# Five units of seven products in the second feed-forward layer, with three sums of weights made in DRAM and the fourth on VectorE

## The chip, the cores and the metric

The kernel runs on one core of a Trainium2 chip. The metric is the device time of one execution in microseconds; the time shown is the median of the runs. Below, PE is TensorE, DVE VectorE, ACT ScalarE, POOL GpSimd, SP SyncE.

## The reference

A bidirectional encoder trunk of two layers on an input of 256 positions by 2048 features, in float32. The first layer mixes by pooling and grouped attention, the second by an mLSTM; each is followed by a gated feed-forward part, which is what the change touches:

```python
D_MODEL = 2048; SEQ = 256; DEPTH = 2; D_FF = 5632

def conv_ffn(x, w_up, conv_w, conv_b, w_down):
    u = x @ w_up                                   # 256 x 2048 by 2048 x 11264
    up = jnp.pad(u, ((0, 0), (1, 1), (0, 0)))
    c = conv_w.astype(u.dtype)
    u = c[0] * up[:, :-2] + c[1] * up[:, 1:-1] + c[2] * up[:, 2:] + conv_b.astype(u.dtype)
    gate, val = jnp.split(u, 2, axis=-1)
    return (jax.nn.silu(gate) * val) @ w_down      # 256 x 5632 by 5632 x 2048

for layer in range(DEPTH):
    h = rms_norm(x, norm_mix[layer])
    ...                                            # attention (layer 0) or mLSTM (layer 1)
    x = x + mixed
    x = x + conv_ffn(rms_norm(x, norm_ffn[layer]), w_up[layer], conv_w[layer], conv_b[layer], w_down[layer])
```

## The kernel before

**Products in two halves.** Every float32 product is made of two-part numbers: activations and weights are each split into a high part (a cast to `fp32r`) and a low part (the rest), and PE makes high x high, high x low and low x high.

**The stream of weights.** All weights stand in one list, `weights`, in the order in which PE uses them. An entry, here called a chunk, is a tile of 128 x 1024 float32, 512 KB. `Stream.load` issues the DMA of the next chunk on SP's queue into a buffer `w`; `Stream.split` makes from it the tile `hl`, with a cast on ACT (L164) and a subtraction on DVE (L165). In a feed-forward layer there are seven buffers `w`, loaded up to seven chunks ahead, and five buffers `hl`, split up to three chunks ahead; the fifth buffer is a pool of its own, used by the chunks whose number leaves 4 when divided by 5. PE's order is the order in which the code is written; that of DVE, ACT, POOL and the DMA queues is set by a scheduler which plays the program through with times of its own, except for instructions that are pinned to their order (`keep_in_program_order`).

**A feed-forward layer.** The 5632 hidden features are 44 tiles of 128, in six groups `c` (`FCH`: 4, 8, 8, 8, 8, 8 tiles). `_ffn_plan` writes the order: an up step `n` (one chunk, 16 matmuls of the tile `up`; four steps make one hidden tile), a down step `d` (one chunk, 12 matmuls, tile `dn`), and a step `s` of a unit. Down steps of group `c - 1` alternate with the up steps of group `c`. A chunk is used by one step, so the steps of a layer number its chunks.

**A unit of seven products.** For four hidden tiles at once (with gate and value, a matrix of 2048 by 1024) `quads` uses the scheme in which a 2 x 2 block product takes seven multiplications instead of eight. It goes through the 16 row blocks of the weights in eight pairs; a pair has four blocks of 128 x 512, called b11, b12, b22 and b21, and needs four sums:

- b11 + b12,
- b12 + b22,
- b22 + (b11 + b12),
- b21 + that.

A unit takes 28 chunks and steps of six matmuls each (tiles `p`; 168 matmuls of 512 columns): 16 in a first pass with two chunks a pair, 12 in a second pass with three chunks for two pairs. PE multiplies sums of the activations (tile `sx`, made by DVE and ACT as each layer begins) and sums of the weights. At its end `finish` transposes the four results (tile `tr`, four transposes for each hidden tile, so 16 in a unit) and passes them to `tail`, the convolution and gate on ACT and DVE.

**Where the sums are made.** `UNITS` lists for each layer the units: group `c`, half of the group, first and last slot (a slot is one step that is not of a unit), and `made`. With `made` 1, all four sums are made in DRAM ahead of time: `make_step` copies the pair's four blocks into a DRAM tile `G` (two copies of 512 KB on SP) and then lets POOL issue accumulating DMAs, two that add from the weights and two within `G`, 256 KB each. Chunks of the unit are then loaded from `G`. With `made` 0, DVE adds in the buffer `w` (`sums`, L144 to L150), four additions of 128 x 512 for each pair. The lists `places` say at the load of which chunk each of a pair's four steps is issued. In each layer the units (2,1), (3,1) and (5,1) have `made` 1 and (4,1) has 0.

Of the kernel before, what the change touches and what calls it, by code (L numbers as in the profile page):

```python
# [64 lines left out]
class Stream:  # L65
# [46 lines left out]
    def make_step(self, key, part, src):  # L112

        pin, sync, add = self.tc.keep_in_program_order, self.nc.sync, self.nc.gpsimd
        G = self.made_tile(key)
        if part < 2:
            r = slice(64 * part, 64 * part + 64)
            pin(sync.dma_start(G[r], src[r]))
            pin(add.dma_start(G[r, 0:1024], src[r, 512:1536], accum_op=ALU.add))  # L119
# [5 lines left out]
    def prepare(self, kind, w):  # L125

        if kind[1] == 0:
            self.first = w
            return
        x, G = self.first, self.made_tile(kind[2])  # L130
        pin, add = self.tc.keep_in_program_order, self.nc.vector.tensor_add
        b11, b12, b22, b21 = (e[:, c : c + 512] for e in (x, w) for c in (0, 512))
        for to, other in ((b11, b12), (b12, b22), (b22, b11), (b21, b22)):
            pin(add(to, to, other))
        self.nc.gpsimd.dma_start(G[:, 0:1024], x)
        self.nc.gpsimd.dma_start(G[:, 1024:2048], w)
# [16 lines left out]
    def split(self, then=None):  # L153
        i = self.n_split
        self.sums(i)
        w, n, width, kind = self.w.pop(i)[:4]
        if isinstance(kind, tuple):
            self.prepare(kind, w)
            self.n_split += 1
            self.sums(i + 1)  # L160
            return
# [18 lines left out]
    def next(self):  # L180
        while self.is_prep(self.at):
            self.at += 1
        i = self.at
        self.ahead(i)
        self.at += 1
        return self.hl.pop(i)

    def is_prep(self, i):
        return isinstance(self.srcs[i], tuple) and isinstance(self.srcs[i][0], tuple)
# [1052 lines left out]
def _down_chunks(w):  # L1242
# [10 lines left out]
    ((2, 1, 18, 57, 1), (3, 1, 64, 90, 1), (4, 1, 97, 141, 0), (5, 1, 148, 174, 1)),  # L1253
# [41 lines left out]
def _ffn_order(layer, up, dn, four, last):  # L1295
# [4 lines left out]
    for step in _ffn_plan(layer):  # L1300
# [7 lines left out]
        else:  # L1308
# [7 lines left out]
            if n >= 2 * m:  # L1316
                seq.append(("made", ((key, 1, 2), q[:, 1024:1536])) if made else ("left", q[:, 512:1536]))
# [7 lines left out]
def _pairs(layer, four):  # L1325
    return [(f"{layer}{c}{h}_{p}", four[u, p]) for u, (c, h, _, _, made) in enumerate(UNITS[layer]) if made
            for p in range(KT // 2)]


def _with_prep(seq, pairs, first, gap):  # L1330

    out = []
    for i, e in enumerate(seq):
        n, r = divmod(i - first, gap)
        if r == 0 and 0 <= n < len(pairs):
            key, q = pairs[n]
            out += [(("prep", 0, key), q[:, 0:1024]), (("prep", 1, key), q[:, 1024:2048])]
        out.append(e)
    return out


def _make_steps(make, pairs, places):

    for (key, q), (at, gap) in zip(pairs, places):
        for part in range(4):
            make.setdefault(at + part * gap, []).append((key, part, q))
# [109 lines left out]
```

## Time and profile before

| | |
|---|---|
| time, median of 3 runs | 2171.28 us (2171.19 to 2171.61) |
| the profiled execution | 2171.85 us, span 2170.1 us |
| PE busy | 2162.6 us, 100% of the span |
| weight loads on PE busy | 1838.7 us, 85% |
| DVE busy | 1679.4 us, 77% |
| ACT busy | 1285.1 us, 59% |
| POOL busy | 185.5 us, 9% |
| moved by DMA | 566.76 MB, mean 261 GB/s |
| granted PE clock | 1.0 |

The times are microseconds from the start of the span. In the trace's answers a row of the timeline gives start, duration, engine, line, operation, the tiles written and read, and the count; what stands in brackets is the idle time before it and what ended it. A row of the windows gives for a stretch of time its length, then the busy time of each engine with the number of instructions, the granted clock, the share of time in which the DMA engines were busy, and the GB/s they moved. Durations of matmuls overlap, since they are pipelined.

The first feed-forward layer is on PE from 256 to 971 us, the mLSTM layer from there to 1449 us, the second feed-forward layer from 1449 us to the end.

### The profile page before, as it was taken

The numbers are of one execution on the slowest core, as the hardware profiler recorded it, in microseconds if no ns is written. First come the engines' busy times: TensorE is split into PE (matmuls) and PEld (weight loads), VectorE is DVE, ScalarE is ACT, GpSimd is POOL, SyncE is SP. The second block draws the span as 40 slices with busy tenths as digits, with TensorE's granted clock in tenths as the row PEclk, the third lists the DMA queues.
The fourth block names the chain that finished last, engine by engine and source line by source line (L and its number), as shares of the span: only waits on it lengthen the run. The fifth ranks groups of instructions, "written<-read, shape, count | busy, mean of one in ns | idle before, by whom it ended". The sixth has DMA issues, their size and how long they took to land.

```text
span 2170.1 us, 30692 instructions
## 1 busy us (share of the span) xinstructions
PE 2162.6 (100%) x11040; PEld 1838.7 (85%) x11040; DVE 1679.4 (77%) x2350; ACT 1285.1 (59%) x1808; POOL 185.5 (9%) x232
## 2 busy tenths in 40 slices
PE   9999999999999999999999999999999999999999
PEld 7888888888888888889888888888888888788887
DVE  7686698787798787866767676769878778878785
ACT  7665565666665566655555454556566665557663
POOL 1121111110101000001111010110000000000000
PEclk9999999999999999999999999999999999999999
DMA  8878889999989978879788887888998997776873
GB/s 325 250 221 254 260 266 341 343 295 313 322 273 306 302 221 255 262 212 254 216 257 228 237 242 224 265 231 250 290 284 268 305 309 241 257 233 223 253 235 125
DMA packets 170268, 566.76 MB, mean 261 GB/s; under 512 B 20762, under 2 KB 23106, under 8 KB 168578
## 3 DMA queue, kind: packets, MB, share of 16 engines
q1 hardware_dynamic: 145376, 510.44, 68.3%
q0 software_dynamic: 21664, 50.61, 15.2%
q10 hardware_dynamic: 3074, 3.75, 0.8%
q8 instruction: 86, 1.41, 0.3%
q14 instruction: 68, 0.56, 0.1%
HBM read 562.57 MB, written 102.80 MB: 307 GB/s over the span
## 4 chain that ended last, share of the span: by engine, by line
PE 98%; DVE 1%; issue 0%; ACT 0%; DMA 0%; ACTq 0%; DVEq 0%
PE up L285 28%; PE dn L285 21%; PE p L285 14%; PE op L285 8%; PE mv L285 4%; PE mq L285 4%; PE mk L285 4%; PE mo L285 4%; PE qproj L285 3%; PE pool L285 1%; PE kproj L285 1%; PE vproj L285 1%; PE tr L1098 1%; PE av L285 1%; PE qk L285 1%; PE end L285 1%
## 5 line engine op out<-in xcount | busy, mean ns | idle before, releaser
L165 DVE TENSOR_TENSOR hl<-w,hl 128x1024 fp32r<-128x1024 f32 (+1 forms) x868 | 1049.8, 1218 | 344.9 <-ACT hl L164 336.7
L164 ACT CAST hl<-w 128x1024 fp32r<-128x1024 f32 (+1 forms) x867 | 902.9, 1049 | 645.7 <-PE up L285 163.4
L285 PE MATMUL up<-xx,hl 128*128 128x512 f32 (+1 forms) x3584 | 650.3, 337 | 0.0
L285 PEld LDWEIGHTS up<-xx,hl 128*128 128x128 f32 x3584 | 566.2, 188 | 88.4
L285 PE MATMUL dn<-hl,g 128*128 128x512 f32 x2064 | 491.8, 391 | 0.0
L285 PEld LDWEIGHTS dn<-hl,g 128*128 128x128 f32 x2064 | 384.9, 188 | 78.4
L285 PE MATMUL p<-hl,sx 128*128 128x512 f32 x768 | 204.5, 390 | 1.5 <-DVE hl L165 0.8
L119 POOL DMA_DIRECT2D G<-in_q x96 | 77.0, 802 | 1177.3 <-DMA G<-in_q 1165.7
L285 PEld LDWEIGHTS p<-hl,sx 128*128 128x128 f32 x768 | 139.2, 188 | 27.6 <-ACT hl L164 1.1
L285 PE MATMUL p<-hl,xx 128*128 128x512 f32 x576 | 156.4, 391 | 0.8 <-DVE hl L165 0.8
L285 PEld LDWEIGHTS p<-hl,xx 128*128 128x128 f32 x576 | 104.2, 188 | 20.7 <-DVE hl L165 1.7
L123 POOL DMA_DIRECT2D G<-G x96 | 89.2, 929 | 258.6 <-DMA G<-in_q 180.8
L285 PE MATMUL mk<-xx,hl 128*128 128x512 f32 (+1 forms) x512 | 92.2, 338 | 0.0
L285 PE MATMUL mq<-xx,hl 128*128 128x512 f32 (+1 forms) x512 | 92.2, 338 | 0.0
L285 PE MATMUL mv<-hl,xx 128*128 128x512 f32 (+2 forms) x480 | 91.8, 350 | 0.0
L285 PE MATMUL op<-hl,cat 128*128 128x512 f32 x384 | 91.6, 394 | 0.0
L285 PE MATMUL mo<-hl,xx 128*128 128x512 f32 x384 | 90.6, 392 | 0.0
L285 PE MATMUL op<-hl,mcat 128*128 128x512 f32 x384 | 89.5, 392 | 0.0
L285 PEld LDWEIGHTS mq<-xx,hl 128*128 128x128 f32 x512 | 79.4, 188 | 11.5
L285 PEld LDWEIGHTS mk<-xx,hl 128*128 128x128 f32 x512 | 79.2, 188 | 11.3
L285 PEld LDWEIGHTS mv<-hl,xx 128*128 128x128 f32 x480 | 78.3, 189 | 11.2
L285 PEld LDWEIGHTS op<-hl,mcat 128*128 128x128 f32 x384 | 71.5, 188 | 14.6
(243 smaller groups left out, 1831.7 us busy)
## 6 DMA issues: line engine op xcount, KB each, us to landing
w<-in_up SPq DMA_DIRECT2D x224, 512.0 KB, 5.3
w<-in_dn SPq DMA_DIRECT2D x176, 512.0 KB, 5.2
w<-in_m_in SPq DMA_DIRECT2D x124, 512.0 KB, 4.8
G<-in_q SPq DMA_DIRECT2D x96, 512.0 KB, 6.3
G<-in_q POOLq DMA_DIRECT2D x96, 256.0 KB, 6.5
G<-G POOLq DMA_DIRECT2D x96, 256.0 KB, 7.5
w<-in_q SPq DMA_DIRECT2D x96, 256.0 KB, 5.2
w<-G SPq DMA_DIRECT2D x96, 256.0 KB, 4.9
```

The lines of the kernel that those rows point to most:

```text
L119: pin(add.dma_start(G[r, 0:1024], src[r, 512:1536], accum_op=ALU.add))
L123: pin(add.dma_start(G[:, at : at + 512], G[:, of : of + 512], accum_op=ALU.add))
L164: (self.nc.vector.tensor_copy if i + c == 0 else self.nc.scalar.copy)(hl[:, 0, c : c + n], w[:, c : c + n])
L165: self.nc.vector.tensor_sub(hl[:, 1, c : c + n], w[:, c : c + n], hl[:, 0, c : c + n].bitcast(F32))
L285: pe.matmul(out_, lhsT, rhs, start=start, stop=stop, skip_group_check=True)
L1098: pe.transpose(tr[:, j, t * P : t * P + P], src[:, c : c + P], ident)
```

## The change

In the second feed-forward layer there are five units, (1,1), (2,1), (3,1), (4,1) and (5,1), each in a shorter stretch of slots, and all of a new kind, `made` 2. Of its four sums three are made in DRAM; the second, b12 + b22, is made by DVE in the buffer `w` (kind `left`, eight additions a unit). So `G` needs only b11, b22 and b21 copied (two copies each of 128 KB and 256 KB on SP) and one block added from the weights (two accumulations of 128 KB on POOL); the two accumulations within `G` stay. The pairs are 40 instead of 24, and `places` of the second layer begins earlier, in the last third of the first feed-forward layer, and is closer set. In group 2 the first down step comes after two hidden tiles instead of one. The plan of the second layer has 324 steps instead of 312: 96 up, 88 down and 140 of units, where there were 112, 88 and 112. The first layer is left as it was. Code that nothing uses (`prepare`, `is_prep`, `_with_prep`) is taken out, which moves the lines: L165 becomes L152, L147 L139, L119 L124, L123 L128, L292 L274.

```diff
-    def make_step(self, key, part, src):
+    def make_step(self, key, full, part, src):
...
         if part < 2:
             r = slice(64 * part, 64 * part + 64)
-            pin(sync.dma_start(G[r], src[r]))
-            pin(add.dma_start(G[r, 0:1024], src[r, 512:1536], accum_op=ALU.add))
+            if full:
+                pin(sync.dma_start(G[r], src[r]))
+                pin(add.dma_start(G[r, 0:1024], src[r, 512:1536], accum_op=ALU.add))
+            else:
+                pin(sync.dma_start(G[r, 0:512], src[r, 0:512]))
+                pin(sync.dma_start(G[r, 1024:2048], src[r, 1024:2048]))
+                pin(add.dma_start(G[r, 0:512], src[r, 512:1024], accum_op=ALU.add))
...
 UNITS = (
     ((2, 1, 18, 57, 1), (3, 1, 64, 90, 1), (4, 1, 97, 141, 0), (5, 1, 148, 174, 1)),
-    ((2, 1, 18, 57, 1), (3, 1, 64, 90, 1), (4, 1, 97, 141, 0), (5, 1, 148, 174, 1)),
+    ((1, 1, 17, 39, 2), (2, 1, 46, 67, 2), (3, 1, 74, 97, 2), (4, 1, 104, 128, 2), (5, 1, 135, 157, 2)),
 )
...
             fill = sum(([*fill[per * b : per * b + per], ("d", c - 1, b)] for b in range(NB)), [])
+            if c == 2 and any(u[:2] == (1, 1) for u in UNITS[layer]):
+                fill = [fill[i] for i in (0, 2, 1, 4, 3, 6, 5, 7)]
...
             if n >= 2 * m:
-                seq.append(("made", ((key, 1, 2), q[:, 1024:1536])) if made else ("left", q[:, 512:1536]))
+                seq.append(("made", ((key, 1, 2), q[:, 1024:1536])) if made == 1 else ("left", q[:, 512:1536]))
...
-    places.append([(at - 182 + 13 * k, 6) for k in range(16)] + [(at + 26 + 20 * k, 10) for k in range(8)])
+    places.append([(at - 236 + 14 * k, 7) for k in range(6)] + [(at - 152 + 9 * k, 4) for k in range(17)]
+                  + [(at + 5 + 12 * k, 6) for k in range(17)])
```

In the names below, `hl572` is the split of chunk 572 of the whole list; the second layer's chunks begin with 554. On PE the first place that differs is chunk 572, the nineteenth of the second layer. Before (three more pairs of `hl572` rows like the two shown stand ahead of the unit's):

```order
L285 MATMUL up1_4_13473<-xx3_8790,hl571_13416 128x256 x2
L285 MATMUL up1_4_13473<-xx3_8790,hl572_13438 128x512 x2
L285 MATMUL up1_4_13473<-xx3_8790,hl572_13438 128x256 x2
L285 MATMUL p1_1_21_13552<-hl573_13477,xx3_8790 128x512 x3
L285 MATMUL p5_1_21_13553<-hl573_13477,sx1_12992 128x512 x3
```

Now, at the same place:

```order
L267 MATMUL up1_4_13583<-xx3_8826,hl571_13526 128x256 x2
L267 MATMUL p1_1_11_13641<-hl572_13548,xx3_8826 128x512 x3
L267 MATMUL p5_1_11_13642<-hl572_13548,sx1_13099 128x512 x3
L267 MATMUL p6_1_11_13654<-hl573_13590,sx1_13099 128x512 x3
L267 MATMUL p4_1_11_13655<-hl573_13590,xx3_8826 128x512 x3
L267 MATMUL up1_4_13583<-xx3_8826,hl574_13614 128x512 x2
```

The unit (1,1) begins here with two steps, where the up steps of the hidden tile went on.

On DVE, in the unit (4,1) of before, the subtraction of chunk 744 (L165) and the additions that it waits for (L149, L150; chunk 744's sums are added up on that of 742):

```order
L165 TENSOR_TENSOR hl743_16804<-w743_16713,hl743_16804 128x1024
L149 TENSOR_TENSOR w744_16736<-w744_16736,w742_16702 128x512
L976 SCALAR_TENSOR_TENSOR y1_23_16773<-tb_up1_23_16769,cst_84,y1_23_16773 128x255 x2
L165 TENSOR_TENSOR hl745_16834<-w745_16747,hl745_16834 128x1024
L150 TENSOR_TENSOR w744_16736<-w744_16736 128x512
L978 SCALAR_TENSOR_TENSOR y1_23_16773<-tb_up1_23_16769,cst_84,y1_23_16773 128x255 x2
L165 TENSOR_TENSOR hl746_16846<-w746_16785,hl746_16846 128x1024
L165 TENSOR_TENSOR hl747_16863<-w747_16802,hl747_16863 128x1024
L165 TENSOR_TENSOR hl744_16817<-w744_16736,hl744_16817 128x1024
```

In the second pass of the new unit (2,1), where DVE makes one sum for a pair (L139):

```order
L139 TENSOR_TENSOR w663_15226<-w663_15226 128x512
L152 TENSOR_TENSOR hl663_15293<-w663_15226,hl663_15293 128x1024
L139 TENSOR_TENSOR w664_15243<-w664_15243 128x512
L152 TENSOR_TENSOR hl665_15326<-w665_15262,hl665_15326 128x1024
L152 TENSOR_TENSOR hl666_15347<-w666_15273,hl666_15347 128x1024
L152 TENSOR_TENSOR hl664_15315<-w664_15243,hl664_15315 128x1024
L152 TENSOR_TENSOR hl667_15358<-w667_15286,hl667_15358 128x1024
```

Before, chunk 744 stood behind three later chunks; now 664 stands behind two, with one addition ahead of it instead of two.

On POOL, around the power of the norm that opens the second feed-forward layer (L292, now L274). Before:

```order
L119 DMA G131_6_12890<-in_q1 64x1024
L123 DMA G131_5_12588<-G131_5_12588 128x512
L119 DMA G131_6_12890<-in_q1 64x1024
L292 TENSOR_TENSOR ry_n3_13072<-rv_n3_13070,mhalf_115 128x2
L123 DMA G131_6_12890<-G131_6_12890 128x512
```

Now:

```order
L124 DMA G131_6_12829<-in_q1 64x512
L128 DMA G131_6_12829<-G131_6_12829 128x512 x2
L124 DMA G131_7_13111<-in_q1 64x512
L274 TENSOR_TENSOR ry_n3_13180<-rv_n3_13178,mhalf_115 128x2
L124 DMA G131_7_13111<-in_q1 64x512
```

The power stood behind the second addition of a pair; it now stands behind the first addition of the next.

More of the change, by code (lines that the diff above doesn't have):

```diff
@@ L123, in make_step @@
             pin(add.dma_start(G[:, at : at + 512], G[:, of : of + 512], accum_op=ALU.add))
[L125 to L136, printed above, removed]
     def sums(self, i):
@@ L155, in split @@
         self.sums(i)
[L156 to L161, printed above, removed]
+        w, n, width = self.w.pop(i)[:3]
         hl = self.home(i, False).tile([P, 2, CH * P], F32R, tag="hl", name=f"hl{i}")
@@ L180, in next @@
     def next(self):
-        while self.is_prep(self.at):
-            self.at += 1
         i = self.at
@@ L186, in next @@
         return self.hl.pop(i)
-    def is_prep(self, i):
-        return isinstance(self.srcs[i], tuple) and isinstance(self.srcs[i][0], tuple)
 class Weave:
@@ L1325, in _pairs @@
 def _pairs(layer, four):
-    return [(f"{layer}{c}{h}_{p}", four[u, p]) for u, (c, h, _, _, made) in enumerate(UNITS[layer]) if made
+    return [(f"{layer}{c}{h}_{p}", made == 1, four[u, p]) for u, (c, h, _, _, made) in enumerate(UNITS[layer]) if made
             for p in range(KT // 2)]
[L1330 to L1339, printed above, removed]
 def _make_steps(make, pairs, places):
-    for (key, q), (at, gap) in zip(pairs, places):
+    for (key, full, q), (at, gap) in zip(pairs, places):
         for part in range(4):
-            make.setdefault(at + part * gap, []).append((key, part, q))
+            make.setdefault(at + part * gap, []).append((key, full, part, q))
 def _constants():
```

## The prediction

> **What bounds the kernel now.** I read the page's first part for the busy shares, then its chain of waits, then the two groups that feed TensorE.
>
> ```profile
> PE 2162.6 (100%) x11040; PEld 1838.7 (85%) x11040; DVE 1679.4 (77%) x2350; ACT 1285.1 (59%) x1808; POOL 185.5 (9%) x232
> ...
> PE 98%; DVE 1%; issue 0%; ACT 0%; DMA 0%; ACTq 0%; DVEq 0%
> ...
> L165 DVE TENSOR_TENSOR hl<-w,hl 128x1024 fp32r<-128x1024 f32 (+1 forms) x868 | 1049.8, 1218 | 344.9 <-ACT hl L164 336.7
> L164 ACT CAST hl<-w 128x1024 fp32r<-128x1024 f32 (+1 forms) x867 | 902.9, 1049 | 645.7 <-PE up L285 163.4
> L285 PE MATMUL up<-xx,hl 128*128 128x512 f32 (+1 forms) x3584 | 650.3, 337 | 0.0
> ...
> L285 PEld LDWEIGHTS p<-hl,sx 128*128 128x128 f32 x768 | 139.2, 188 | 27.6 <-ACT hl L164 1.1
> ```
>
> PE is busy for all but 7.5 us and is 98% of the chain that ended last. The first two groups are the split: every 512 KB chunk of weights becomes a high and a low half by an ACT cast (1.049 us) and a DVE subtraction (1.218 us), and PE needs both. So a change pays if it shortens what PE must do, and costs if a split comes late. Next I asked what PE waited for in the second feed-forward layer (from 1449 us to the end).
>
> ```profile
> engine line waited for: us in total, times, longest us
> PE p L285 <- DVE hl L165: 1.6, 3, 0.8
> PE p L285 <- ACT hl L164: 0.7, 1, 0.7
> ```
>
> All of it, 2.3 us, stands before `p` matmuls, the seven-product units, and on the split.
>
> **What a step costs on PE.** The timeline inside unit (3,1), starts in the first column:
>
> ```profile
> 1700.03 2.88 PE L285 MATMUL dn<-hl,g 128*128 128x512 f32 x12
> 1702.75 0.84 PE L285 MATMUL p<-hl,sx 128*128 128x512 f32 x3
> 1703.43 0.84 PE L285 MATMUL p<-hl,xx 128*128 128x512 f32 x3
> 1704.11 2.94 PE L285 MATMUL up<-xx,hl 128*128 128x512 f32 x16
> 1706.89 0.85 PE L285 MATMUL p<-hl,xx 128*128 128x512 f32 x3
> 1707.58 0.84 PE L285 MATMUL p<-hl,sx 128*128 128x512 f32 x3
> 1708.26 2.94 PE L285 MATMUL up<-xx,hl 128*128 128x512 f32 x16
> ```
>
> From start to start, a down step of 12 matmuls takes 1702.75 - 1700.03 = 2.72 us; an up step of 16 takes 1706.89 - 1704.11 = 2.78; a unit's step of six takes 1708.26 - 1706.89 = 1.37 and 1704.11 - 1702.75 = 1.36, so 1.365. These are what I sum; the busy time of the groups overlaps and would mislead. The finish of a unit adds transposes:
>
> ```profile
> 1644.55 3.64 PE L285 MATMUL up<-xx,hl 128*128 128x512 f32 x20
> 1648.02 0.60 PE L1098 MATMUL tr<-cst,c 128*128 128x128 f32 x4
> 1648.38 5.14 PE L285 MATMUL up<-xx,hl 128*128 128x512 f32 x28
> 1653.36 0.60 PE L1098 MATMUL tr<-cst,c 128*128 128x128 f32 x4
> 1653.71 3.06 PE L285 MATMUL up<-xx,hl 128*128 128x512 f32 x16
> 1656.60 1.54 PE L285 MATMUL dn<-hl,g 128*128 128x512 f32 x6
> ```
>
> Between 1644.55 and 1656.60 (12.05 us) stand 64 up matmuls, four steps, 11.12 us, and two groups of four transposes: 0.93 us, 0.465 a group.
>
> **The change, part by part.**
>
> *The fifth unit.* Four hidden tiles are no longer made by 16 up steps but by one unit of 28 steps and four groups of transposes: -16 x 2.78 = -44.48, +28 x 1.365 = +38.22, +4 x 0.465 = +1.86. Sum -4.40 us, all on PE's path. The order of the program confirms the counts.
>
> A rule speaks for a larger gain. The Trainium skill, "Perfetto Trace Analysis", section "Identifying the Most-Contended Engine", says that the busy share of matmuls does not tell how near TensorE is to its limit, and that MFU and the busy share of weight loads do. By it the sum would go by loads, of which 256 fall away and 168 + 16 come; rival 4 has its price.
>
> *The unit without made sums disappears.* Unit (4,1) makes all its sums on DVE. These are its stalls on PE:
>
> ```profile
> 1821.33 0.39 PE L285 MATMUL p<-hl,xx 128*128 128x512 f32 x1
> 1821.99 0.74 PE L285 MATMUL p<-hl,xx 128*128 128x512 f32 x2 [0.27 <-DVE hl L165]
> 1822.56 0.85 PE L285 MATMUL p<-hl,sx 128*128 128x512 f32 x3
> 1823.25 1.07 PE L285 MATMUL dn<-hl,g 128*128 128x512 f32 x4
> ...
> 1854.91 0.39 PE L285 MATMUL p<-hl,xx 128*128 128x512 f32 x1
> ...
> 1857.14 1.09 PE L285 MATMUL up<-xx,hl 128*128 128x512 f32 x5
> ...
> 1879.19 2.88 PE L285 MATMUL dn<-hl,g 128*128 128x512 f32 x12
> 1882.79 0.49 PE L285 MATMUL p<-hl,sx 128*128 128x512 f32 x1 [0.73 <-ACT hl L164]
> 1884.06 0.73 PE L285 MATMUL p<-hl,sx 128*128 128x512 f32 x2 [0.77 <-DVE hl L165]
> ...
> 1885.32 1.98 PE L285 MATMUL dn<-hl,g 128*128 128x512 f32 x8
> ```
>
> Step for step: 1823.25 - 1821.33 = 1.92 against 1.365 (0.55 lost), 1857.14 - 1854.91 = 2.23 (0.86), 1882.79 - 1879.19 = 3.60 against 2.72 (0.88), 1885.32 - 1882.79 = 2.53 (1.16). Together 3.45 us. In the order of before each of these places is one where the subtraction of a chunk stands on DVE behind those of one to three later chunks, because the chunk's own sum was due: 717 and 718 behind 719, 732 and 733 behind 734, 744 behind 745, 746 and 747. With the unit these go: -3.45 us.
>
> *What new stalls come.* All five units now have one sum on DVE for every pair of weight blocks, eight a unit.
>
> ```profile
> L147 DVE TENSOR_TENSOR w<-w 128x512 f32<-128x512 f32 x8 | 5.5, 684 | 0.0
> ```
>
> An addition costs 0.684 us, so 8 x 0.684 = 5.5 us a unit; 40 in the layer where there were 32. The order of the changed kernel has late subtractions again: eight chunks behind one later chunk, two (664 and 674) behind two, and 732 and 733 behind 734. How much does that cost? In the first layer the same four-sum unit has six chunks behind one later chunk, and between 600 and 760 us:
>
> ```profile
> core 0: us, PE busy (x) PEld busy (x) DVE busy (x) ACT busy (x) POOL busy (x), PEclk, DMA share, GB/s
> 310.00:446.00 136.00, 136.00 (x710) 116.33 (x709) 108.33 (x137) 84.60 (x108) 19.76 (x25) 1.00 1.02 336
> 600.00:760.00 160.00, 160.00 (x797) 135.53 (x796) 135.88 (x176) 90.43 (x112) 15.39 (x19) 1.00 0.93 291
> 1672.00:1780.00 108.00, 108.00 (x528) 91.18 (x527) 83.13 (x94) 65.14 (x75) 8.14 (x10) 1.00 0.95 304
> 1802.00:1958.00 156.00, 153.67 (x756) 128.76 (x755) 128.23 (x161) 84.29 (x102) 4.07 (x5) 1.00 0.77 248
> ```
>
> PE is busy 160.00 of 160 there, so a chunk behind one costs nothing. The kind "one pair behind one later" cost 0.55 and 0.86 above, but there another addition (0.684) stood in between on DVE, and in the changed order it does not, nor for 664 and 674. Worked out: PE frees the buffer of the later chunk, then has a unit step and a full step left, 1.365 + 2.72 = 4.09 us; cast, subtraction, subtraction need 1.049 + 2 x 1.218 = 3.49 us, and with the addition 4.17. So 4.17 met 4.09 and lost 0.55 to 0.86, that is 0.5 to 0.8 of hidden delay; 3.49 + 0.8 = 4.29 would lose 0.2. Three places: 0 to 2.6 us, and I take 0.6, near the worked value.
>
> Load on DVE is the other side. The row of 1672:1780 is unit (3,1): 53 splits x 1.218 = 64.6 of 83.13 us, 18.5 of other work, 77% of the time. The new units are denser: unit (2,1) has 28 unit steps and 20 others, 38.2 + 20 x 2.75 = 93 us of PE, in which DVE has 47 x 1.218 = 57.2, about 18.5 and 5.5: 81 us, 87%. Unit (1,1) has 49 splits (59.7), gates five hidden tiles where (3,1) gates seven (some 15 us of other work) and holds ten operations on the sums of activations, about 6.8 at 0.684 each: with the 5.5 these are 87 of 96 us, 91%. The nearest rows with that load are 600:760 (135.88 of 160, 85%, no loss) and 1802:1958 (128.23 of 156, 82%, 2.33 us idle). So between 0 and 2.3 us for each of the first two units; nearer to the first row, since an equal load lost nothing where no chunk was late by more than one. I take 0.4 in all. New stalls: 0.6 + 0.4 = +1.0 us, bounds 0 and 2.6 + 4.6 = 7.2.
>
> *Making the sums in DRAM.* A pair is copied in 768 KB instead of 1 MB, four copies on SP instead of two, and its first addition on POOL is halved; 40 pairs instead of 24. Take the densest stretch: unit (1,1) loads 48 chunks (25.2 MB) while four pairs are made at 1.57 MB each: 31.5 MB in about 98 us, 321 GB/s. The row 310:446 is a unit of the first layer with more making beside it: DMA share 1.02, 336 GB/s for 136 us, PE busy 136.00. A full DMA queue is hidden there by the prefetch of seven chunks, so I cost it at 0; without that cover every load would come later by what its share lacks (rival 3). Each pair's first use comes 68 chunks or more after its copies, over 90 us even if all were unit steps. SP gets 112 more copies and 4 more loads to issue, on a queue that issues ahead by the depth of the buffers. On POOL the `rsqrt` powers stand between the accumulations. The one before the second layer:
>
> ```profile
> 1447.50 0.79 POOL L119 DMA_DIRECT2D G<-in_q  x1 [13.31 <-DMA G<-in_q]
> 1452.79 0.71 POOL L292 TENSOR_TENSOR ry_n<-rv_n,mhalf 128x2 f32<-128x2 f32 x1 [4.49 <-DVE rv_n L290]
> ```
>
> In before it stands behind the second addition of its pair, issued with load 6 of the layer, and then waits 4.49 us for DVE. In the change it stands behind the first addition of a pair, issued with load 5, so it should not be later; if it were, the row's 13.31 us wait for a copy, less the 4.49 of cover, is what TensorE could meet once.
>
> *ACT* gets 12 casts more (12.6 us over 714, on an engine at 59%); nothing waits on it alone.
>
> **Sum.** -4.40 - 3.45 + 1.0 = -6.85 us. On the profiled execution 2171.85 (span 2170.1) this gives 2165.0; the median of the runs is 2171.28, 0.57 lower, so 2164.4. A measurement of this kernel tells about 0.2%, 4.3 us, from no change.
>
> **Rivals.**
> 1. *The late splits eat the gain.* DVE at 87 to 91% in two units that follow each other: if each of these two loses what unit (4,1) lost (3.45), 6.9 us come back and the time is 2171.28 - 7.85 + 6.9 = 2170.3. For it: the loss appeared in one layer and not in the other at the same density, so small shifts decide. Against it: the long inversions are gone.
> 2. *Every sum chains DVE and ACT (slower).* A chunk with a sum can be cast only after the addition, so subtraction, addition, cast and subtraction could run one after the other: 0.684 + 1.049 = 1.73 us per sum in which DVE splits nothing. Forty of them, uncovered, are 69 us, a quarter 17 us: 2180.7. It decides from 7.85 / 40 = 0.2 us a sum. Against it: the two four-sum units of before have 32 sums each, and the 64 cost 3.45 us, 0.05 each.
> 3. *DMA is the bound in the units.* If the makings held the rate down to the 291 GB/s of row 600:760, 31.5 MB would take 108 us instead of 98 in the first unit; five such units less the gain give 2171.3 + 50 - 7.85, about 2213. It decides at 31.5 MB in 99.6 us, 316 GB/s. Against it: 336 GB/s at 1.02 without loss.
> 4. *TensorE goes by weight loads.* Then the unit saves 72 x 0.188 = 13.5 us instead of 4.40, and the time is 2171.28 - 13.5 - 3.45 + 1.0 = 2155.3. The 0.188 us is the last group quoted from the page. Against it: in 1802:1958, PEld is busy 128.76 us for 755 loads, 0.171 each, beside 153.67 of matmul; and the six matmuls of a step follow each other at 0.2275 us, which is longer than a load. So PE goes by columns, not by weights. The trace does not bear out what the Trainium skill's rule would give here.
>
> **How the numbers follow.** The forecast (new stalls under 3.5 us, 2163.4 to 2166.9): 0.74. Rival 1 (stalls of 3.5 to 9 us): 0.16. Rival 2: 0.05. Rival 3: 0.03. Rival 4: 0.02. Predicted 2164.4. The range reaches from 2162.8 (no new stall, and 0.6 us of what the median may lie off the profile) to 2170.0 (nearly all of the upper bound of 7.2 us: 2163.4 + 6.6); about 0.84 lie in it. Faster by over 0.2% (under 2166.9): 0.74 + 0.02 = 0.76. Within: 0.15. Slower: rivals 2 and 3 and what is left of 1, 0.09.
>
> **What would show it.** Right: up matmuls fall from the 3584 of the page to 3328 and `p` rises by 168, with the unit's steps still at 1.365 us; the waits of PE in the second layer stay under 2.5 us and stand at the chunks 664, 674 and 732, if anywhere; the span falls by some 7 us. DVE's share in the units rises towards 0.9. Wrong: waits of PE on `hl` in units (1,1) and (2,1) of several us (rival 1), waits at each sum (rival 2), ACT waiting for DMA on `w` (rival 3), or a step of six under 1.3 us (rival 4).

## The result, and the profile after

The changed kernel takes 2165.92 us (median of 11 runs, 2163.8 to 2169.82) against 2171.39 beside it (11 runs, 2171.19 to 2173.05): a ratio of 0.9975, interval 0.9967 to 0.9983, so 5.5 us faster. The runs of the change spread over 6 us, those of before over 2; the profiled execution is the shortest of them, 2163.8 us with a span of 2162.0. The prediction was 2164.4 with a range of 2162.8 to 2170.0: the sign and the range hold, one of the three places forecast for stalls was met, and one term of the sum was too small.

The page of the changed kernel, in the parts that were shown of before:

```profile
PE 2156.9 (100%) x10968; PEld 1831.9 (85%) x10968; DVE 1693.7 (78%) x2367; ACT 1298.6 (60%) x1824; POOL 237.5 (11%) x296
...
PE 98%; DMA 1%; DVE 1%; issue 0%; ACT 0%; SPq 0%; ACTq 0%; DVEq 0%
...
L152 DVE TENSOR_TENSOR hl<-w,hl 128x1024 fp32r<-128x1024 f32 (+1 forms) x880 | 1062.6, 1218 | 333.7 <-ACT hl L151 324.5
L151 ACT CAST hl<-w 128x1024 fp32r<-128x1024 f32 (+1 forms) x879 | 914.3, 1049 | 643.6 <-PE up L267 136.8
L267 PE MATMUL up<-xx,hl 128*128 128x512 f32 (+1 forms) x3328 | 605.5, 337 | 0.0
...
L267 PE MATMUL p<-hl,sx 128*128 128x512 f32 x864 | 227.3, 390 | 0.1
...
L267 PE MATMUL p<-hl,xx 128*128 128x512 f32 x648 | 174.7, 390 | 0.0
```

The matmuls are as counted: `up` falls to 3328, `p` is 864 + 648 = 1512, nine units of 168 where there were eight (768 + 576). PE stays at 98% of the chain; its idle time falls from 7.5 to 2162.0 - 2156.9 = 5.1 us.

PE's waits in the whole execution, by what was waited for (total, times, longest):

```profile
PE wps L291 <- DVE pad L660: 1.2, 1, 1.2
```

The only one left is at the start of the program. In the second feed-forward layer the view lists none, where before had 2.3 us.

The windows of the new units (1,1), (2,1), (3,1) and (4,1) (length, busy time of PE, PEld, DVE, ACT and POOL, clock, DMA share, GB/s):

```profile
1512.00:1608.00 96.00, 96.00 (x483) 81.45 (x482) 83.57 (x107) 61.46 (x78) 13.62 (x17) 1.00 1.01 329
1632.00:1720.00 88.00, 87.88 (x420) 73.45 (x419) 74.65 (x88) 54.95 (x64) 11.36 (x14) 1.00 1.00 331
1720.00:1850.00 130.00, 130.00 (x644) 109.74 (x643) 107.73 (x139) 83.99 (x109) 16.25 (x20) 1.00 0.98 309
1850.00:1975.00 125.00, 125.00 (x621) 105.58 (x620) 105.05 (x137) 79.88 (x103) 5.66 (x7) 1.00 0.84 272
```

The same stretch as the second row, in before:

```profile
1632.00:1720.00 88.00, 88.00 (x446) 74.63 (x445) 72.91 (x99) 57.26 (x76) 6.50 (x8) 1.00 0.90 279
```

Here is the price of the change. Making sums raises the DMA share of this stretch from 0.90 to 1.00 and the rate from 279 to 331 GB/s, and DVE has 74.65 us of work in 88. In unit (1,1) both are as high (1.01, 329 GB/s, 83.57 of 96) and PE loses nothing; (3,1) and (4,1) have DVE at 83 and 84% and PE full. The 0.12 us that PE lacks in the second row are in unit (2,1). The timeline of PE there, and of its weight loads:

```profile
1703.57 1.52 PE L267 MATMUL p<-hl,xx 128*128 128x512 f32 x6
1704.93 2.88 PE L267 MATMUL dn<-hl,g 128*128 128x512 f32 x12
1707.65 3.29 PE L267 MATMUL p<-hl,sx 128*128 128x512 f32 x12
1710.78 1.53 PE L267 MATMUL dn<-hl,g 128*128 128x512 f32 x6
...
1709.51 0.99 PEld L267 LDWEIGHTS p<-hl,sx 128*128 128x128 f32 x5 [0.54 <-DVE hl L152]
```

The two steps that begin at 1707.65 take 1710.78 - 1707.65 = 3.13 us instead of 2.73: 0.40 lost, on the split of chunk 674, one of the two that the order showed behind two later ones. A unit's step still takes 1704.93 - 1703.57 = 1.36.

The end of the last matmul tells what PE's work came to, free of what follows it. The last group of matmuls in before, and then in the change (start and duration):

```profile
2155.09 11.04 PE L285 MATMUL end<-hl,g 128*128 128x512 f32 x48
```

```profile
2149.83 8.55 PE L267 MATMUL end<-hl,g 128*128 128x512 f32 x37
```

2155.09 + 11.04 = 2166.13 against 2149.83 + 8.55 = 2158.38: 7.75 us earlier. The first two terms of the sum were 7.85.

### The profile page after: what moved, and what is told of

It is laid out like the page before. It is cut to its first block, busy times and chain, and to the rows that moved or that the text cites. A ratio compares the mean times of both kernels' runs of the same rounds, so it can differ in the third digit from the quotient of the medians.

```text
span 2162.0 us, 30888 instructions
## 1 busy us (share of the span) xinstructions
PE 2156.9 (100%) x10968; PEld 1831.9 (85%) x10968; DVE 1693.7 (78%) x2367; ACT 1298.6 (60%) x1824; POOL 237.5 (11%) x296
## 4 chain that ended last, share of the span: by engine, by line
PE 98%; DMA 1%; DVE 1%; issue 0%; ACT 0%; SPq 0%; ACTq 0%; DVEq 0%
PE up L267 26%; PE dn L267 21%; PE p L267 15%; PE op L267 8%; PE mv L267 4%; PE mq L267 4%; PE mk L267 4%; PE mo L267 4%; PE qproj L267 3%; PE pool L267 1%; PE vproj L267 1%; PE kproj L267 1%; PE tr L1080 1%; PE qk L267 1%; PE av L267 1%; PE end L267 1%
## 5 line engine op out<-in xcount | busy, mean ns | idle before, releaser
L152 DVE TENSOR_TENSOR hl<-w,hl 128x1024 fp32r<-128x1024 f32 (+1 forms) x880 | 1062.6, 1218 | 333.7 <-ACT hl L151 324.5
L151 ACT CAST hl<-w 128x1024 fp32r<-128x1024 f32 (+1 forms) x879 | 914.3, 1049 | 643.6 <-PE up L267 136.8
L267 PE MATMUL up<-xx,hl 128*128 128x512 f32 (+1 forms) x3328 | 605.5, 337 | 0.0
L267 PEld LDWEIGHTS up<-xx,hl 128*128 128x128 f32 x3328 | 526.2, 188 | 82.7
L267 PE MATMUL p<-hl,sx 128*128 128x512 f32 x864 | 227.3, 390 | 0.1
L267 PEld LDWEIGHTS p<-hl,sx 128*128 128x128 f32 x864 | 157.5, 188 | 30.1 <-DVE hl L152 0.5
L267 PE MATMUL p<-hl,xx 128*128 128x512 f32 x648 | 174.7, 390 | 0.0
L128 POOL DMA_DIRECT2D G<-G x128 | 116.4, 910 | 377.0 <-DMA G<-in_q 234.8
L267 PEld LDWEIGHTS p<-hl,xx 128*128 128x128 f32 x648 | 117.7, 188 | 21.6
L124 POOL DMA_DIRECT2D G<-in_q x80 | 65.1, 814 | 625.3 <-DMA G<-in_q 606.7
L120 POOL DMA_DIRECT2D G<-in_q x48 | 38.1, 793 | 432.8 <-DMA G<-in_q 421.9
```

The lines of the kernel that those rows point to most:

```text
L124: pin(add.dma_start(G[r, 0:512], src[r, 512:1024], accum_op=ALU.add))
L151: (self.nc.vector.tensor_copy if i + c == 0 else self.nc.scalar.copy)(hl[:, 0, c : c + n], w[:, c : c + n])
L152: self.nc.vector.tensor_sub(hl[:, 1, c : c + n], w[:, c : c + n], hl[:, 0, c : c + n].bitcast(F32))
L267: pe.matmul(out_, lhsT, rhs, start=start, stop=stop, skip_group_check=True)
```

## The experiments

The theory after this result: the two terms on PE are right, and the spread comes from unit (2,1), where loads land late beside the copies that make sums, on a DVE that has no room to catch up, ahead of the late subtraction of 674. The rivals: the late subtraction alone does it; or DVE's additions alone; or DMA alone. The runs were made on four chips (e0 to e3, e4 to e6, e7 and e9, e10 to e12), each beside runs of the kernel before; of these four the changed kernel itself ran on the first alone (e0), so across chips only the ratios compare; the line numbers are those of the changed kernel.

### e0: the changed kernel again

No edit.

> The changed kernel once more, for the spread of its runs: they went from 2163.8 to 2169.8 us while those of the kernel before went from 2171.2 to 2173.1. All theories: a median of 2164.5 to 2167.5 us and single runs up to some 2170 again. Theory DMA (loads come late in the units because the making of sums fills the DMA queues, and PE then stalls a varying number of times) expects a longer run's trace to show PE or ACT waiting for loads of w. Theory late split (the subtractions that stand behind later ones lose a varying time) expects PE waiting for hl at chunks 664, 674 and 732 with the loads long landed. Theory chip (nothing in the kernel) expects the kernel before to vary as much beside it.

Measured: 2167.45 us (2165.08 to 2169.31, 11 runs) against 2171.41 (21 runs), 0.998 (0.9971 to 0.9989). Its runs spread over 4.2 us, those of the kernel before beside it over 1.9, so the chip alone is not the cause. Its profiled execution is the median run, 2167.45 with a span of 2165.6, and shows the stall in full. The list of PE's waits in the layer holds one, 2.0 us for DVE's `hl` ahead of `p`. The timeline of PE at chunk 674:

```profile
1707.58 1.88 PE L267 MATMUL p<-hl,sx 128*128 128x512 f32 x7
1711.48 1.43 PE L267 MATMUL p<-hl,sx 128*128 128x512 f32 x5 [2.02 <-DVE hl L152]
1712.74 4.51 PE L267 MATMUL dn<-hl,g 128*128 128x512 f32 x12
1717.09 1.53 PE L267 MATMUL p<-hl,xx 128*128 128x512 f32 x6
```

From 1707.58 to 1712.74 two unit steps take 5.16 us instead of 2.73; then the twelve matmuls of a down step, which wait for nothing, take 1717.09 - 1712.74 = 4.35 instead of 2.72. The windows of PE (length, busy time, granted clock, DMA share, GB/s) tell why:

```profile
1690.00:1709.00 19.00, 19.00 (x93) 1.00 0.96 300
1709.00:1712.00 3.00, 0.98 (x4) 1.00 1.00 303
1712.00:1717.00 5.00, 5.00 (x16) 0.66 0.99 338
1717.00:1730.00 13.00, 13.00 (x63) 1.00 0.97 326
```

The granted clock is 0.66 in the five microseconds after the stall and 1.00 on both sides. So 2.43 us of stall cost 1.63 more: 4.06 us, against the 0.40 of the execution above, and 2165.6 - 2162.0 = 3.6 is what the spans differ by.

How the stall comes about, from SP, ACT and DVE (start, duration, operation, and in brackets the wait ahead of it):

```profile
1688.57 0.59 SPq L122 DMA_DIRECT2D G<-in_q  x1
1689.21 0.58 SPq L123 DMA_DIRECT2D G<-in_q  x1
1689.89 0.58 SPq L100 DMA_DIRECT2D w<-in_b  x1
```

```profile
1698.99 1.05 ACT L151 CAST hl<-w 128x1024 fp32r<-128x1024 f32 x1 [2.85 <-DMA w<-in_b]
```

```profile
1700.08 1.23 DVE L152 TENSOR_TENSOR hl<-w,hl 128x1024 fp32r<-128x1024 f32 x1 [2.49 <-ACT hl L151]
...
1707.93 3.49 DVE L152 TENSOR_TENSOR hl<-w,hl 128x1024 fp32r<-128x1024 f32 x3
```

The load `in_b` is that of chunk 671. It uses the buffer that chunk 664 frees, whose subtraction is the other late one, so on SP it stands behind the loads of 672 and 673 and behind two copies into `G`. It is issued at 1689.89, and ACT waits 2.85 us for it until 1698.99, over 9 us later, where the page gives a median of 5.7 us from issue to landing for `in_dn`. DVE then idles 2.49 us. From 1700.08 on it has no gap in the trace until 1711.42, when the last of three subtractions in a row (675, 676, then 674) ends; PE resumes at 1711.48. The 2.49 us were never made up.

ACT was free for this cast at 1698.99 - 2.85 = 1696.14, so the load had 6.25 us to land, and it took 9.10. The same two rows in the shorter execution above:

```profile
1689.88 0.53 SPq L100 DMA_DIRECT2D w<-in_b  x1
```

```profile
1697.03 1.05 ACT L151 CAST hl<-w 128x1024 fp32r<-128x1024 f32 x1 [0.82 <-DMA w<-in_b]
```

The load was issued at the same time and took 7.15 us. The two executions differ by how long this transfer took, not by when it was issued.

### e1: without the making

```diff
-                seq.append(("made", ((key, 2, 4),)) if made else ("chain", q[:, 1024:2048]))
+                seq.append(("made", ((key, 2, 4) if made == 1 else q[:, 1024:2048],)) if made else ("chain", q[:, 1024:2048]))
...
-                seq.append(("made", (q[:, 0:512], (key, 0, 1))) if made else ("sum", q[:, 0:1024]))
+                seq.append(("made", (q[:, 0:512], (key, 0, 1) if made == 1 else q[:, 512:1024])) if made else ("sum", q[:, 0:1024]))
...
-    ... for u, (c, h, _, _, made) in enumerate(UNITS[layer]) if made
+    ... for u, (c, h, _, _, made) in enumerate(UNITS[layer]) if made == 1
```

In the second layer no sums are made in DRAM: the copies and accumulations are left out, and the chunks are loaded straight from the weights. PE's and DVE's work and its order stay.

> The making of the second layer's sums is left out: no copies into G and no accumulations for that layer, and the unit's chunks are loaded from the weights themselves, in the same number of loads of the same size, so the products are of other numbers. Order, splits and the 40 additions on DVE stay. Theory DMA: 2163.4 us (the forecast without any new stall), spread under 1 us. Theory late split: 2164 to 2167 us and the same spread as the changed kernel. Theory chip: the same as the changed kernel.

Measured: 2163.53 us (2163.43 to 2163.64, 5 runs), 0.9963 (0.9949 to 0.9976). No wait of PE in the layer. Its spread is 0.2 us, and its slowest run is below the fastest of e0 on the same chip: 3.9 us at the median go with the making, though the late subtractions are all still there. That rules out the late subtraction alone, and the additions alone, which stay too.

### e2: without the additions

```diff
-                seq.append(("made", ((key, 1, 2), q[:, 1024:1536])) if made == 1 else ("left", q[:, 512:1536]))
+                seq.append(("made", ((key, 1, 2), q[:, 1024:1536]) if made == 1 else (q[:, 512:1536],)) if made else ("left", q[:, 512:1536]))
```

The 40 additions on DVE are left out; the making stays as it is.

> The 40 additions on DVE in the second layer are left out: the chunk with b12 and b22 is loaded as it is and not summed. The making in DRAM stays. Theory DMA: median and spread as the changed kernel, 2164.5 to 2167.5. Theory late split: no subtraction is late any more, 2163.4 us, spread under 1 us.

Measured: 2163.48 us (2163.34 to 2163.55, 5 runs), 0.9962 (0.995 to 0.9975), no wait of PE. So DMA alone does not do it either. Between 1690 and 1710 us, first e2, then e0, then e5 (below) and e1:

```profile
1690.00:1710.00 20.00, 20.00 (x98) 16.80 (x96) 15.91 (x18) 13.12 (x16) 2.40 (x3) 1.00 0.99 325
```

```profile
1690.00:1710.00 20.00, 19.46 (x93) 15.93 (x91) 15.63 (x20) 12.03 (x15) 2.18 (x3) 1.00 0.96 296
```

```profile
1690.00:1710.00 20.00, 20.00 (x96) 16.64 (x96) 17.95 (x23) 13.02 (x16) 2.46 (x3) 1.00 0.92 287
```

```profile
1690.00:1710.00 20.00, 20.00 (x97) 16.67 (x96) 17.97 (x23) 13.21 (x16) 0.00 (x0) 1.00 0.80 257
```

With the additions DVE has 17.95 of 20 us to do where PE runs full, so 2.05 us of room; without them 15.91, 4.09 of room, at a DMA share of 0.99. By this count a late load that idles DVE for 2.49 us does not fit into the one and fits into the other. The run does not separate this from a second effect: with no late subtraction of 664, SP issues the load of 671 earlier. In e2:

```profile
1684.21 0.33 SPq L100 DMA_DIRECT2D w<-in_b  x1
```

That is 5.68 us earlier than in e0, and ACT does not wait for it.

### e3: the four old units

```diff
-    ((1, 1, 17, 39, 2), (2, 1, 46, 67, 2), (3, 1, 74, 97, 2), (4, 1, 104, 128, 2), (5, 1, 135, 157, 2)),
+    ((2, 1, 18, 57, 2), (3, 1, 64, 90, 2), (4, 1, 97, 141, 2), (5, 1, 148, 174, 2)),
```

The second layer has the four units of before in their old slots, all with three sums in DRAM and one on DVE: the unit (4,1) without made sums goes, the fifth unit does not come.

> The second layer keeps the four units and their slots of the kernel before, but all four are of the new kind (three sums in DRAM, one on DVE). This takes away the unit whose sums DVE made, and adds no fifth unit. My sum: before less 3.45 us of stalls, 2167.9 us, plus up to 0.5. Theory late split expects a spread of 1 us or less, since the units are less dense (DVE at some 80%); theory DMA expects a spread of 1 to 2 us, with 32 pairs made instead of 40. If the stalls of unit (4,1) had nothing to do with its sums, it would come out at 2171.3.

Measured: 2169.47 us (2169.36 to 2170.8, 11 runs), 0.9991 (0.9982 to 0.9999), 1.6 above the sum's 2167.9. PE has no wait in the layer, and its last matmuls are:

```profile
2151.61 11.04 PE L267 MATMUL end<-hl,g 128*128 128x512 f32 x48
```

2151.61 + 11.04 = 2162.65, which is 3.48 us earlier than before, where the sum had 3.45. The rest was lost behind it: from there to the end of the span are 2167.7 - 2162.65 = 5.05 us, in before 3.97, in the change 3.62. In this tail, and in neither of the other two, stands a fetch of instructions (queue, packets, MB, share):

```profile
q14 instruction: 1, 0.01, 0.4%
```

Its place fits, but no run tested that it makes the difference: why the tail is longer stays open. Ten of the 11 runs lie within 0.4 us; the eleventh is the 2170.8.

### e4 and e6: the splits pinned to program order

```diff
+            pin = self.tc.keep_in_program_order if i >= 572 else (lambda e: e)
-            (self.nc.vector.tensor_copy if i + c == 0 else self.nc.scalar.copy)(hl[:, 0, c : c + n], w[:, c : c + n])
+            pin((self.nc.vector.tensor_copy if i + c == 0 else self.nc.scalar.copy)(hl[:, 0, c : c + n], w[:, c : c + n]))
...
+            pin(self.nc.vector.tensor_sub(...))
```

From chunk 572 on, casts and subtractions keep the order in which the code is written, so none is late. In e6 with fewer makings besides (the places of e5).

> Casts and subtractions of the second layer's chunks from 572 on are pinned to the order of the chunks, so that none stands behind a later one; loads, makings and the 40 additions stay. The trace of the longer run showed one stall, at chunk 674, behind 675 and 676, after two casts that waited for loads. Theory order (the late subtraction is needed for the stall): 2163.5 us, spread under 1 us. Theory DMA alone (the load is late, whatever the order): 2164.5 to 2167.5 with the spread of the changed kernel. If pinning makes DVE wait at the additions: 2165 or more in every run.

> Both edits together: order pinned and making moved. All theories: 2163.4 us in every run, spread under 0.5 us, no wait of TensorE in the second layer; better than both kernels. If either edit costs something of its own, it shows here against the other two.

Measured: 2256.51 us (2247.62 to 2257.84), 1.038 (1.0363 to 1.0397), and for e6 2253.25 (2248.32 to 2254.8), 1.0371 (1.0357 to 1.0385). Both are some 90 us longer than the same kernels without the pinning; of the expectations only the third of e4 holds, 2165 or more. The waits of e4 in the layer (the lines stand one lower in this kernel, L152 being the cast):

```profile
PE p L268 <- ACT hl L152: 15.3, 11, 3.4
PE dn L268 <- ACT hl L152: 14.0, 8, 4.1
```

```profile
ACT hl L152 <- DVE w L139: 67.7, 28, 4.2
```

ACT now stands in line for the additions, 67.7 us, and PE for ACT. PE's waits in the layer, for ACT and DVE, are 51.7 us in all, and a mean clock of 0.986 over a span of 2254.7 us comes to some 31 us more. Pinning did not take away two late subtractions; it changed the whole order of two engines. The runs say what that freedom of order is worth here, some 90 us, and nothing on the late subtraction.

### e5 and e12: fewer makings in the second layer

```diff
-    places.append([(at - 236 + 14 * k, 7) for k in range(6)] + [(at - 152 + 9 * k, 4) for k in range(17)]
-                  + [(at + 5 + 12 * k, 6) for k in range(17)])
+    places.append([(at - 236 + 14 * k, 7) for k in range(6)] + [(at - 152 + 8 * k, 4) for k in range(20)]
+                  + [(at + 12 + 16 * k, 6) for k in range(14)])
```

Of the 40 pairs, 26 instead of 23 are made ahead of the layer, and those within it every 16 chunks instead of every 12. Order on DVE and late subtractions stay. e12 is the same kernel on the chip of e10 and e11.

> The order is left as the scheduler makes it (674 behind 675 and 676), but the making is moved: 20 instead of 17 pairs in the mLSTM stage, a pair for 8 chunks there, and 14 instead of 17 in the second feed-forward layer, a pair for 16 chunks instead of 12. Theory both needed (late load and late subtraction): 2163.5 us, spread under 1 us, since the loads of chunks 671 to 676 land earlier. Theory order alone: as the changed kernel, 2164.5 to 2167.5.

> The kernel with less making in the second feed-forward layer once more, beside the two shifted ones: 2163.4 to 2164.0 us in every run, all theories.

Measured: e5 2163.72 us (2163.49 to 2163.9, 5 runs), 0.9962 (0.995 to 0.9975); e12 2163.66 (2163.46 to 2165.88, 5 runs), 0.9965 (0.9952 to 0.9977). No wait of PE in the layer in either. The window of unit (2,1), and the load of 671 on SP, in e5:

```profile
1632.00:1720.00 88.00, 88.00 (x422) 73.70 (x420) 74.94 (x89) 55.04 (x64) 8.94 (x11) 1.00 0.95 312
```

```profile
1689.64 0.33 SPq L100 DMA_DIRECT2D w<-in_b  x1
```

DMA share 0.95 instead of 1.00 and no copies directly ahead of the load: with the same work on DVE (74.94 us) PE waits for nothing, as the theory that both are needed expected. Which of the two differences does it, the runs don't separate: e11 has the copies there and has no wait of PE in the layer either, at a DMA share of 0.99. One run of e12 misses its expectation with 2165.88; it is the profiled one, and its loss lies elsewhere, in the mLSTM, where more is now made:

```profile
1020.34 2.59 PE L267 MATMUL mk<-xx,hl 128*128 128x256 f32 x14 [2.15 <-DVE hl L152]
```

```profile
1015.22 0.35 DVE L828 SCALAR_TENSOR_TENSOR arg<-G,mc,kml 128x128 f32<-128x128 f32 x1 [2.39 <-DMA G<-gd]
1017.41 1.15 DVE L828 SCALAR_TENSOR_TENSOR arg<-G,mc,kml 128x256 f32<-128x256 f32 x3 [1.83 <-DMA G<-gd]
...
1019.07 1.22 DVE L152 TENSOR_TENSOR hl<-w,hl 128x1024 fp32r<-128x1024 f32 x1
```

PE waits 2.15 us for a split whose subtraction starts on DVE at 1019.07, behind two waits for a small transfer of the mLSTM's own (`gd`), 2.39 and 1.83 us. That the makings moved there cause it is not shown: e11, which makes no more in the mLSTM than the change, also has PE wait at `mk`, 0.8 us.

### e7: one addition less

```diff
+                plain = layer == 1 and u == 1 and at == 7
-                seq.append(("made", ((key, 1, 2), q[:, 1024:1536])) if made == 1 else ("left", q[:, 512:1536]))
+                seq.append(("made", ((key, 1, 2), q[:, 1024:1536])) if made == 1 else
+                           ("made", (q[:, 512:1536],)) if plain else ("left", q[:, 512:1536]))
```

The addition of the pair of chunk 674 is left out; its subtraction is then no longer late behind two.

> One of the 40 additions on DVE is left out, that of chunk 674 (the last pair of unit (2,1)); 39 stay, and all of the making. In the order 674 then stands ahead of 675 and 676, and only 673 stands behind one chunk. If the stall needs this one late subtraction: 2163.4 to 2163.8 us in every run, and no wait of TensorE. If late loads and a full DVE do it whatever the order: median 2164.5 to 2167 and a spread of 2 us or more.

Measured: 2164.52 us (2163.68 to 2165.26, 5 runs), 0.9965 (0.9953 to 0.9978). The first expectation is missed; of the second the median is just met and the spread, 1.6 us, is not. The stall moves to the chunk before, 673, and is smaller:

```profile
1708.45 2.79 PE L267 MATMUL p<-hl,sx 128*128 128x512 f32 x11 [0.44 <-DVE hl L152]
```

ACT waited 3.0 us for the load of 671 in this execution, as long as in e0. So late loads stall PE without that late subtraction too; the same lateness cost 0.44 us of waiting here and 2.02 with it. (The edit also takes 0.68 us of work off DVE, and the run does not separate the two.)

### e9: more makings in the second layer

```diff
-    ... [(at - 152 + 9 * k, 4) for k in range(17)] + [(at + 5 + 12 * k, 6) for k in range(17)]
+    ... [(at - 152 + 11 * k, 4) for k in range(14)] + [(at + 3 + 10 * k, 5) for k in range(20)]
```

> The order of DVE is the change's, and the making in the second feed-forward layer is set closer: 20 pairs there, one for 10 chunks (the change: 17, one for 12; the kernel with less making: 14, one for 16, 2163.7 us), and fewer in the mLSTM stage. If making that fills the DMA queues sets how late the loads are: 2168 us or more, stalls in more runs and more places than in the change. If only the presence of making matters: 2164.5 to 2167.5 as the change.

Measured: 2164.96 us (2163.89 to 2166.53, 6 runs), 0.9968 (0.9956 to 0.998), in the profiled run a wait of 0.8 us at chunk 674. The DMA share of 1632 to 1720 us is 1.01, at 336 GB/s.

The expectation of a dose, 2168 us or more, is missed: with more making than in the change the ratio is no worse (0.9968 against 0.9975 and 0.998, with intervals that overlap).

### e10 and e11: the makings shifted

```diff
-                  + [(at + 5 + 12 * k, 6) for k in range(17)])
+                  + [(at + 8 + 12 * k, 6) for k in range(17)])
```

The makings within the layer come three chunks later (e10) or six (e11, with 11 in place of 8), their number as in the change. In e11 copies stand again directly ahead of the load of 671.

> As many pairs are made in the second feed-forward layer as in the change, one for 12 chunks, but each three chunks later, so that the copies into G no longer stand on SP's queue directly ahead of the load of chunk 671, whose buffer comes free late because the subtraction of 664 stands behind two others. If this one load, behind these copies, makes the stall: 2163.5 to 2164.0 us in every run, as with less making. If the amount of making does: 2164.5 to 2168 as the change.

> The control of the shift: six chunks later, which with copies every six chunks puts them at the same chunks again, ahead of the load of 671, only of another pair. If the place of the copies counts: 2164.5 to 2168 and a spread of 2 us or more, as the change. If only the shift as such mattered: 2163.5 to 2164.0.

Measured: e10 2164.46 us (2164.03 to 2167.36, 5 runs), 0.9966 (0.9952 to 0.9979); e11 2164.01 (2163.39 to 2165.41, 5 runs), 0.9965 (0.9952 to 0.9978). What the place of the copies was to do is missed in both: the shift that should have helped has a run with the full stall, the one that should not have helped is shorter. The wait of e10:

```profile
1711.42 1.98 PE L267 MATMUL p<-hl,sx 128*128 128x512 f32 x5 [2.02 <-DVE hl L152]
```

So copies directly ahead of that load are not enough to cause it, nor is their absence enough to avoid it. The traces of all these runs, one execution each, say what the stall goes with. The first column is when the load of 671 was issued, counted from the layer's first matmul; the second is from there to the start of the cast that waited for it; the last is PE's time from that matmul to the end of the layer's last:

| execution | issued, us | landed after, us | ACT waited for it, us | layer on PE, us |
|---|---|---|---|---|
| the change | 240.2 | 7.15 | 0.82 | 708.7 |
| e9 | 239.7 | 8.33 | 1.51 | 709.4 |
| e10 | 239.7 | 9.55 | 2.74 | 712.2 |
| e0 | 240.3 | 9.10 | 2.85 | 712.4 |
| e7, one addition less | 240.2 | 9.30 | 2.98 | 709.0 |
| e11 | 240.2 | in time | 0 | 708.4 |
| e5, e12 | 239.7 | in time | 0 | 708.4 |
| e1, no making | 239.7 | in time | 0 | 708.4 |
| e2, no additions | 234.5 | in time | 0 | 708.3 |

Wherever this load is in time the layer takes 708.3 to 708.4 us. Where it is late the layer is longer, by more the later it is while all additions stay (in e10 and e0 a part of that is the clock's). Copies directly ahead move its issue by half a microsecond only; what varies is how long the transfer takes, and what decides that in a single run stays open. The changed kernel itself was not run on this chip, so that a part of the difference to e0 can be the chip's.

## Why the prediction was right, and where not

- *The fifth unit, -4.40.* Right. The last matmul ends at 2162.65 without it (e3) and 4.36 earlier with it and no stall, in e5:

```profile
2149.74 8.55 PE L267 MATMUL end<-hl,g 128*128 128x512 f32 x37
```

2149.74 + 8.55 = 2158.29. Counted from the layer's first matmul (1449.74 in e3, 1449.90 in e5) it is 4.52.

- *The unit (4,1), -3.45.* Right: 3.48 (e3), or 3.61 counted from the layer's first matmul (1449.61 in before).
- *DVE's load, +0.4.* Right in that it costs nothing by itself: e1 keeps it and has no wait. Unit (1,1), forecast at 91%, has 83.57 of 96 us, 87%, with a DMA share of 1.01, and PE is busy 96.00. What the mean over a unit hid is the stretch of 1690 to 1710 us, with 90%.
- *Late subtractions, +0.6.* The place was right for one of three, chunk 674; nothing was lost at 664, 732 and 733. The working, which took only ACT and DVE times, gave 0.2 a place; the loss was 0.40 in one profiled execution and 4.06 in the other, of which 1.63 were the clock's. With loads in time (e1, e5) the step of 674 lost 0.1 us. Two counts of the working are one chunk short: the plan has 48 chunks from the first to the last step of unit (2,1), not 47, and 49 of unit (1,1), for which the DMA sum has 48. They shift DVE's share in (2,1) and the rate in (1,1) by some 2% and change no term.
- *Making in DRAM, 0.* This is the step that failed. "A full DMA queue is hidden there by the prefetch of seven chunks" was read from row 310:446 of the first layer, whose unit makes all sums in DRAM, so that DVE adds nothing there and can catch up. In unit (2,1) the load of 671 is issued only after the late subtraction of 664, has 6.25 us to land and takes 7.15 to 9.55 in five of the six profiled executions with as much making in the layer as the change or more, while DVE has 2 us of room. (That late loads and the additions are both needed is what e1, e2 and e5 agree on; no run brought that load forward with all else left.) The median of the change stands 2.4 us above e1, e2 and e5 (2163.5 to 2163.7), that of e0 3.9; the sum had +1.0 for all new stalls.
- *The sum.* -4.40 - 3.45 + 2.4 is -5.45, and 2165.92 - 2171.39 = -5.47 was measured. Since the 2.4 is counted from e1, e2 and e5, this says no more than that these come out at the 2163.4 us which the two PE terms give.
- *The rivals.* Rival 1 is the nearest to what was missed: late splits gave back 2 to 6 us in the longer runs, but in the profiled executions at one chunk, not over two units. Rival 2 is out: 40 sums, no wait at any of them but one. Rival 3's sign was there, ACT waiting for DMA (e0: five waits in the layer, 8.4 us in all), but only the one of 2.85 us goes with a wait of PE: the DMA share is 0.98 to 1.01 in three units and bounds none. Rival 4 is out: PE's end moved by 7.75, near the 7.85 by columns and far from the 13.5 + 3.45 by loads.

The best version here is e5's placing of the makings: 2163.72 and 2163.66, ten runs, nine of them within 2163.46 to 2163.93. Its intervals overlap that of the change (0.9967 to 0.9983), and the change was not run on those two chips, so that it is better than the change is told by the runs' spread and not proven; beside it on the same chip, e11 is at 2164.01.

## What to carry to other kernels

A transfer that was hidden in one stage is hidden in another only if it is issued early enough there and the engine that takes it in has room to catch up: compare the busy share over a stretch of some 20 us around the late place, not the mean of a stage. Where work moves off an engine onto DMA, keep the DMA share below full where DVE has no room (here the load was in time at 0.95 and 0.97, and late in five of six executions at 0.98 to 1.01), and look in the order of the transfers for a load whose buffer a late subtraction frees. A profile of one execution can be the best of its kind: the spread of the runs is what shows a stall that is there only at times.

## What the hardware showed

A wait of 2.02 us on PE was followed by half the granted clock. In e10, where it came again (above), the two microseconds from 1713 us read 0.50:

```profile
1711.00:1713.00 2.00, 1.58 (x5) 0.77 0.91 225
1713.00:1715.00 2.00, 2.00 (x6) 0.50 0.88 213
1715.00:1717.00 2.00, 2.00 (x9) 0.88 1.04 380
```

The three rows come to 2 x 0.23 + 2 x 0.50 + 2 x 0.12 = 1.7 us of lost clock, so 3.4 us at half. The wait of 2.15 us in e12 had no such sequel (clock 1.00 in the rows of 2 us after it), nor had the short waits of before, 0.73 and 0.77 us. The Trainium skill, "TensorE: Matmul & The Clock Gate", section "Why this matters for your kernels", advises to leave no gaps of more than about 3 us between matmuls; in these two runs a shorter one was enough. Of the 22 runs of the change, the 11 that took 2167.3 us or more have a mean clock of 0.998 or 0.999, and the 11 up to 2166.1 have 1.0, so the step of over a microsecond between the two groups goes with the clock. A mean of 0.999 alone shows no stall: the profiled execution of e3 has it without a wait of PE in the layer, from its tail, where PE is idle and the clock reads 0.50.
